# Layer A's attention: the output bank copied once and its crossed halves turned by DMA and added by GpSimd, a long row's minimum carried from one piece to the next, and small operations moved or dropped

## The chip, the cores and the metric

The kernel runs on one core of one Trainium2 chip. A core has five engines with queues of their own: TensorE (PE: matrix products and transposes; PEld is its loading of weights), VectorE (DVE), ScalarE (ACT), GpSimd (POOL) and SyncE (SP), which here issues nearly all DMAs. Each engine works through its queue in order, and an instruction that waits for a semaphore holds up everything behind it on that engine. The metric is the device time of one execution in microseconds, the median of several runs; lower is better.

## What is computed

A causal decoder of two layers on 1024 tokens of width 1024, in float32. Layer A attends in three ways and mixes them by gates; layer B attends with dilated windows over a shared K and V; each layer ends in a SwiGLU feed-forward part. The change lies in layer A's attention alone. Cut to what matters:

```
q: 16 heads of 64, K and V: 4 groups (4 heads share one), scale 1/8
o_cmp = softmax(q k_cmp + bias) v_cmp          # 63 compressed blocks of keys
imp   = sum over the 4 heads of p_cmp, per block of 64 keys
sel   = the 8 best blocks of a query (first, own and previous one forced)
o_sel = softmax(q k[sel] + bias) v[sel]        # causal
o_win = softmax(q k[last 256] + bias) v[last 256]
o     = g0 * o_cmp + g1 * o_sel + g2 * o_win   # g = sigmoid(gate logits)
x     = x + o @ w_out
```

A softmax here takes the row's maximum off first. The kernel keeps negated scores (the factor -1/8 is in q, the bias is stored negated), so the row's maximum is a minimum, and ACT forms exp(minimum - score).

## The kernel before, in words

**Stages.** The program runs through: projections of layer A (to about 290 us), layer A's attention (about 290 to 750), its output projection and feed-forward part (to about 1450), the shared K and V and layer B's queries, layer B's attention (about 1927 to 2230), its output projection and feed-forward part. All products keep float32 accuracy: a value is split into a rounded part (`h`) and the rest (`l`), and two or three fast products take the place of one slow one. Where a tile is used whole, one slow product (line L296) does it.

**Layer A's attention.** The work is cut into 32 units (g, t): 4 groups of heads by 8 blocks of 128 queries, the group on the outside. A unit has five jobs: `cmp_job` (compressed blocks, 4 heads, and for t >= 4 the choice of blocks) and four `dense_job`s: window (br = 2) and selected (br = 1), each for two heads (hp = 0, 1). A job has a front and a back, and `pipelined` puts a job's back two jobs behind its front.

- The front of `dense_job`: PE forms the scores of a head (L675, L676; `s`, three PSUM banks), DVE adds the bias, writes `P` and takes the minimum of the row in one instruction (L678). A row of over 512 keys (br = 1, t >= 4) comes in two pieces, n - 512 and 512 keys; the minima of both go into `mp`, and L682 takes the smaller one. ACT forms the exponentials and their sum (L684), DVE the reciprocal (L686), GpSimd multiplies by it and by the gate (L688).
- The back: PE turns blocks of `P` (L275, `pt`, three banks), ACT copies the result rounded (`th`, L138), DVE forms the rest (`tl`, L139), and PE adds the product with V into the unit's output bank (`o`, two banks; L297, L298). Some blocks go another way, to take load off DVE: a plain copy out of PSUM (L289, by ACT for hp = 0, by DVE for hp = 1), and GpSimd makes `th` and `tl` (L290, L291). And the window's first two blocks for hp = 1 are copied whole (`whole`, L281, by ACT) and used in the slow product L296.
- `cmp_job` has small steps on DVE: the sum is held above 1e-30 (L614), the reciprocal (L615), for t = 0 a mask (L617), the product with the gate (`dg`, L619); GpSimd multiplies `pc` by it (L623).
- At the end of a unit `evac_o` empties the output bank. It holds 64 columns of V's rounded part and 64 of its rest, so that for every second head the two 64-partition halves have to be crossed and added: ACT copies one half of the bank to the other partitions (L308, 64x256), DVE adds the other half to it (L309); both twice per unit. The sum goes into `oT`, which the output projection reads.

**What sets the order.** Instructions are put on the engines by a scheduler that goes by its own costs and by the order in which the program was written; so an edit in one place can move instructions elsewhere. Loads for a group (Q, K, KW, V, VW, T) are issued by SP when a slot of their ring is free, most of them at a change of group. The output projection's weights `ow` and its input `xr` are loaded by the same queue, into memory that the attention gives back.

Of the kernel before, what the change touches and what calls it, by code (L numbers as in the profile page):

```python
# [10 lines left out]
F32 = mybir.dt.float32  # L11
# [3 lines left out]
OP = mybir.AluOpType  # L15
# [76 lines left out]
def trunk(ctx, tc, I, out):  # L92
    nc = tc.nc
# [206 lines left out]
    cp_a, cp_v = nc.scalar.copy, nc.vector.tensor_copy  # L300
# [214 lines left out]
    oT = pool(oT_ctx, "oTa", "right").tile([128, KC, S], F32, name="oT")  # L515

    with ExitStack() as c:
        kB = pool(c, "aB")
        wk = pool(c, "aw")
# [16 lines left out]
        grp = {}  # L536
# [50 lines left out]
        gt = lambda g, t, br, h0, n: gates[:, t, 12 * g + 3 * h0 + br:12 * g + 3 * (h0 + n):3]  # L587
        tok = lambda t: slice(t * 128, (t + 1) * 128)

        def query(g, t, hh):  # L590
            return grp["Q", g, t // 4, hh][:, tok(t % 4)]

        def cmp_job(g, t):
# [17 lines left out]
            for hh in range(4):  # L611
                nc.scalar.activation(pc[:, hh, :nv], pc[:, hh, :nv], AF.Exp, bias=mx[:, hh:hh + 1], scale=-1.0,
                                     accum_out=dn[:, hh:hh + 1])
            nc.vector.tensor_scalar(dn, dn, 1e-30, None, op0=OP.max)  # L614
            nc.vector.reciprocal(dn, dn)  # L615
            if t == 0:
                nc.vector.tensor_scalar(dn, dn, crow, None, op0=OP.mult)  # L617
            dg = wk.tile([128, 4], F32, name="dg", bufs=3)
            nc.vector.tensor_mul(dg, dn, gt(g, t, 0, 0, 4))  # L619
            if t >= 4:  # L620
                pn = wk.tile([128, 4, 64], F32, name="pn", bufs=2)
                nc.gpsimd.tensor_mul(pn[:, :, :nv], pv, dn[:].unsqueeze(2).to_broadcast([128, 4, nv]))
# [25 lines left out]
                nc.tensor.matmul(po, vc[:, g, :], tl, start=False, stop=False, skip_group_check=True)  # L648
            return back

        def dense_job(g, t, br, hp):

            k0 = max(t - 2, 0) if br == 2 else 0
            nb = t + 1 - k0
            n = 128 * nb
            P = wk.tile([128, 2, 1024 if br == 1 else 384], F32, name=f"P{br}", bufs=4)
            mm = wk.tile([128, 2], F32, name="m", bufs=8)
            sm = wk.tile([128, 2], F32, name="sm", bufs=8)
            masked = br == 1 and t >= 4
            kh, kl = grp["K", g] if br == 1 else grp["KW", g, t // 4]  # L660
            skip = 256 if br == 2 and t >= 4 else 0
            cuts = [(0, n - 512, 0), (n - 512, n, 1)] if n > 512 else [(0, n, 1)]
            mp = wk.tile([128, 2, 2], F32, name="mp", bufs=4) if len(cuts) == 2 else None
            for e in range(2):
                hh = 2 * hp + e
                q = query(g, t, hh)
                for i, (lo, hi, a) in enumerate(cuts):
                    bias = grp["T", g, a, hh] if br == 1 else grp["TW", g, hh]
                    ps = bank("s")
                    w, rw = max(hi - lo, 256), hi - lo  # L670
                    ks = slice(k0 * 128 - skip + lo, k0 * 128 - skip + lo + w)

                    nr = 128 if br == 2 else 80 if masked else 64
                    ql = grp["QM", g][:, hh, tok(t - 4)] if masked else q
                    nc.tensor.matmul(ps[:, :w], q, kh[:, ks], start=True, stop=False)  # L675
                    nc.tensor.matmul(ps[:, :w], ql[:nr], kl[:nr, ks], start=False, stop=True)  # L676
                    bs = slice(bias.shape[-1] - rw, bias.shape[-1])
                    nc.vector.tensor_tensor_reduce(  # L678
                        out=P[:, e, lo:hi], in0=ps[:, :rw], in1=bias[:, bs], scale=1.0, scalar=3e38, op0=OP.add,
                        op1=OP.min, accum_out=mm[:, e:e + 1] if len(cuts) == 1 else mp[:, e, i:i + 1])  # L680
            if len(cuts) == 2:
                nc.vector.tensor_tensor(mm, mp[:, :, 0], mp[:, :, 1], op=OP.min)  # L682
            for e in range(2):
                nc.scalar.activation(P[:, e, :n], P[:, e, :n], AF.Exp, bias=mm[:, e:e + 1], scale=-1.0,  # L684
                                     accum_out=sm[:, e:e + 1])
            nc.vector.reciprocal(sm, sm)  # L686
            for e in range(2):
                nc.gpsimd.tensor_scalar(P[:, e, :n], P[:, e, :n], sm[:, e:e + 1], gt(g, t, br, 2 * hp + e, 1),  # L688
                                        op0=OP.mult, op1=OP.mult)

            def back():
                po = po_[g, t]
                for b0 in range(0, nb, 2):
                    bs = range(b0, min(b0 + 2, nb))
                    th, tl = transposed(wk, [P[:, e, b * 128:(b + 1) * 128] for b in bs for e in range(2)],
                                        (cp_a, cp_v)[hp] if br == 2 and b0 == 2 else None,
                                        whole=cp_a if br == 2 and hp == 1 and b0 == 0 else None)
                    for i, b in enumerate(bs):
                        last = br == 1 and b == nb - 1
                        cs = slice(i * 256, (i + 1) * 256)  # L700
                        o_ = po[:, hp * 256:(hp + 1) * 256]
                        v_ = grp["V", br - 1, g, (k0 + b) // 4][:, (k0 + b) % 4, :]
                        mm_pv(o_, v_, th, tl, cs, False, last)
                if br == 1 and hp == 1:
                    evac_o(wk, po, oT[:, 2 * g:2 * g + 2, tok(t)])
            return back

        def jobs():
# [955 lines left out]
```

## Time and profile before

| | us |
|---|---|
| median of 3 runs (lowest, highest) | 3033.9 (3033.78, 3038.08) |
| the profiled execution, first to last instruction | 3035.7 |
| PE, DVE, ACT, POOL busy in it | 2899.3, 2401.7, 1603.6, 1630.1 |
| mean granted TensorE clock | 0.983 |

The page gives no device time of the profiled execution beside its span. The span lies within the spread of the runs, so what lies around it is smaller than that spread.

How to read the views. A row of the groups is: line, engine, operation, what is written and read, count | busy us, mean ns of one | idle us of the engine just before these instructions, and what ended it. A row of the waits is: who waited, for whom, us in total, times, longest us. A row of the windows gives each engine's busy time in a stretch, with the number of instructions. A row of the timeline is: start, duration, engine, line, operation, count, and in brackets the idle time ahead of it. "PEld" rows are loads of weights; since PE's queue is in order, a weight load that waits holds PE up.

### The profile page before, as it was taken

What the parts mean: (1) busy time and instruction counts of PE and PEld (TensorE: products, weight loads), DVE (VectorE), ACT (ScalarE), POOL (GpSimd) and SP (SyncE); (2) the same over time, 40 slices, a digit from 0 to 9 for tenths busy, and PEclk for the clock granted to TensorE, in tenths of its full rate; (3) what the DMA queues carried; (4) which work ended last, traced back from release to release, by engine and by line L of the source; (5) the groups of instructions that cost most, each with busy time, mean ns of one, the idle gap of its engine ahead of it and who ended that gap; (6) DMA issues with size and microseconds to landing.
All of it is one profiled execution on the core that took longest, in us unless ns stands there. A gap on an engine that the chain in (4) does not pass through costs nothing.

```text
span 3035.7 us, 44147 instructions
## 1 busy us (share of the span) xinstructions
PE 2899.3 (96%) x14670; PEld 2381.4 (78%) x14670; DVE 2401.7 (79%) x4832; ACT 1603.6 (53%) x3596; POOL 1630.1 (54%) x1751
## 2 busy tenths in 40 slices
PE   7999999999889999999999999899988899999997
PEld 6987888888677877777777778788866787777776
DVE  4432888988988888888876677589899788888887
ACT  5432888887463333333364444689965433333334
POOL 2134666666766555555556787333357755555551
PEclk9999999999999999999999999999999999999999
DMA  6765032121112222222124555876420211112111
GB/s 167 223 191 165 25 103 78 36 56 70 60 53 63 63 67 74 65 59 70 56 95 141 160 160 145 264 209 179 138 94 25 66 55 57 56 46 62 51 45 73
DMA packets 266196, 293.43 MB, mean 97 GB/s; under 512 B 17971, under 2 KB 209347, under 8 KB 265968
## 3 DMA queue, kind: packets, MB, share of 16 engines
q1 hardware_dynamic: 246320, 230.45, 26.3%
q0 software_dynamic: 19648, 60.16, 6.6%
q8 instruction: 116, 1.90, 0.3%
q14 instruction: 112, 0.92, 0.1%
HBM read 227.44 MB, written 78.81 MB: 101 GB/s over the span
## 4 chain that ended last, share of the span: by engine, by line
PE 68%; DVE 16%; ACT 5%; issue 4%; DMA 4%; POOL 2%; SPq 1%; DVEq 0%; ACTq 0%; POOLq 0%
PE ux L165 5%; PE ux L166 5%; PE ux L167 5%; PE uy L166 4%; PE uy L165 4%; PE uy L167 4%; DVE pl L762 4%; PE pt L275 4%; PE dx L166 3%; PE dr L165 3%; PE dx L167 3%; PE dx L165 3%; PE dr L166 3%; PE dr L167 3%; PE mm L165 3%
## 5 line engine op out<-in xcount | busy, mean ns | idle before, releaser
L762 DVE TENSOR_TENSOR pl<-oT,ph 128x512 fp32r<-128x512 f32 x315 | 325.2, 1052 | 41.3 <-ACT ph L761 35.4
L761 ACT ACTIVATE ph<-oT 128x512 fp32r<-128x512 f32 x329 | 199.0, 626 | 228.1 <-PE ux L166 65.8
L275 PE MATMUL pt<-ident,P 128*128 128x128 f32 x1536 | 245.1, 278 | 11.0 <-ACT P L1458 2.7
L761 ACT ACTIVATE ph<-oTb 128x512 fp32r<-128x512 f32 x239 | 143.2, 625 | 189.4 <-PE ux L166 55.7
L762 DVE TENSOR_TENSOR pl<-oTb,ph 128x512 fp32r<-128x512 f32 x229 | 224.4, 1005 | 23.5 <-ACT ph L761 23.4
L820 DVE TENSOR_TENSOR xr<-xr,dr 128x512 f32<-128x512 f32 x336 | 214.6, 679 | 33.9 <-PE dr L167 33.8
L139 DVE TENSOR_TENSOR tl<-pt,th 128x512 fp32r<-128x512 f32 (+1 forms) x320 | 207.1, 651 | 33.8 <-ACT th L138 31.9
L820 DVE TENSOR_TENSOR xr<-xr,dx 128x512 f32<-128x512 f32 x352 | 220.3, 678 | 3.6 <-PE dx L167 2.4
L166 PE MATMUL dx<-pl,ph 128*128 128x512 f32 x512 | 203.4, 401 | 9.7 <-DVE pl L762 9.0
L688 POOL TENSOR_SCALAR P<-P,sm,gates 128x384 f32<-128x384 f32 (+7 forms) x256 | 183.5, 728 | 53.4 <-DVE sm L686 48.0
L275 PEld LDWEIGHTS pt<-ident,P 128*128 128x128 f32 x1536 | 179.8, 142 | 30.0 <-ACT P L1458 6.7
L138 ACT ACTIVATE th<-pt 128x512 fp32r<-128x512 f32 (+1 forms) x320 | 177.2, 563 | 44.3 <-PE pt L275 40.4
L167 PE MATMUL dx<-ph,pl 128*128 128x512 f32 x512 | 200.0, 397 | 0.3 <-DVE pl L762 0.3
L684 ACT ACTIVATE P<-P,m 128x384 f32<-128x384 f32 (+7 forms) x256 | 170.7, 669 | 16.1 <-DVE m L682 8.4
L1081 POOL TENSOR_TENSOR oT<-oT,gffn 128x512 f32<-128x512 f32 x92 | 105.9, 1158 | 136.2 <-DMA oT<-in_ffn_w_up_dram 110.5
L165 PE MATMUL dx<-ph 128*128 128x512 f32 x512 | 157.3, 400 | 6.7 <-DVE xr L820 3.3
L1081 POOL TENSOR_TENSOR oTb<-oTb,gffn 128x512 f32<-128x512 f32 x92 | 106.4, 1165 | 99.1 <-DMA oTb<-in_ffn_w_up_dram 77.0
L298 PE MATMUL o<-tl,V 128*128 128x256 f32 x540 | 148.8, 299 | 7.4 <-POOL tl L291 3.7
L297 PE MATMUL o<-th,V 128*128 128x256 f32 x540 | 151.4, 296 | 2.7 <-ACT th L138 1.4
L290 POOL TENSOR_SCALAR th<-traw 128x128 fp32r<-128x128 f32 (+1 forms) x112 | 75.1, 674 | 129.3 <-ACT traw L289 47.7
L1458 ACT ACTIVATE P<-P,st 128x384 f32<-128x384 f32 (+2 forms) x256 | 139.6, 547 | 7.6 <-PE pt L1569 4.1
L166 PEld LDWEIGHTS dx<-pl,ph 128*128 128x128 f32 x512 | 97.6, 191 | 39.5 <-DVE pl L762 19.4
(617 smaller groups left out, 9582.4 us busy)
## 6 DMA issues: line engine op xcount, KB each, us to landing
qB<-xr POOLq DMA_DIRECT2D x96, 256.0 KB, 4.7
oT<-in_ffn_w_up_dram SPq DMA_DIRECT2D x92, 256.0 KB, 3.0
oTb<-in_ffn_w_up_dram SPq DMA_DIRECT2D x92, 256.0 KB, 3.0
Q<-qB SPq DMA_DIRECT2D x40, 512.0 KB, 7.0
wd<-in_ffn_w_down_dram SPq DMA_DIRECT2D x66, 256.0 KB, 2.6
oT<-in_b_w_q_dram SPq DMA_DIRECT2D x48, 256.0 KB, 3.5
K<-kBs SPq DMA_DIRECT2D x40, 256.0 KB, 9.5
wraw<-in_a_w_in_dram SPq DMA_DIRECT2D x18, 512.0 KB, 4.9
```

The costliest lines, as they stand in the source:

```text
L138: nc.scalar.activation(H_, src, AF.Copy)
L139: nc.vector.tensor_sub(L_, src, f32(H_))
L165: nc.tensor.matmul(ps, lh, rh, start=first, stop=False, skip_group_check=bool(shared))
L166: nc.tensor.matmul(ps, lh, rl, start=False, stop=False, skip_group_check=bool(shared))
L167: return nc.tensor.matmul(ps, ll, rh, start=False, stop=last, skip_group_check=bool(shared))
L275: nc.tensor.transpose(ps[:, i * 128:(i + 1) * 128], b, ident)
L684: nc.scalar.activation(P[:, e, :n], P[:, e, :n], AF.Exp, bias=mm[:, e:e + 1], scale=-1.0, accum_out=sm[:, e:e + 1])
L688: nc.gpsimd.tensor_scalar(P[:, e, :n], P[:, e, :n], sm[:, e:e + 1], gt(g, t, br, 2 * hp + e, 1), op0=OP.mult, op1=OP.mult)
L761: nc.scalar.activation(h, src, AF.Copy)
L762: (eng or nc.vector).tensor_sub(l, src, f32(h))
L820: nc.vector.tensor_add(xs, xs, banks[t])
L1081: nc.gpsimd.tensor_mul(v, v, gains[:, k:k + 4].unsqueeze(2).to_broadcast([128, 4, 128]))
```

## The change

Five edits, all in layer A's attention:

1. `evac_shifted` takes the place of `evac_o` (which layer B keeps). ACT copies the whole bank to SBUF in one instruction (`oraw`, 128x512, one buffer); SP issues two DMAs of 64x256 that put each crossed half on its partitions (`oturn`, two buffers); GpSimd adds each half (64x256, both inputs in SBUF) into `oT`.
2. A row of two pieces: the minimum of the first piece is the start value of the second piece's instruction, so that its result is the row's minimum. L682 is gone. The pieces are now on the outside of the loop and the two heads inside.
3. `dg` is formed by GpSimd.
4. The bound of 1e-30 is kept for t = 0 only.
5. The whole copy of the window's first two blocks (hp = 1) goes from ACT to DVE.

```diff
-            nc.vector.tensor_scalar(dn, dn, 1e-30, None, op0=OP.max)
+            if t == 0:
+                nc.vector.tensor_scalar(dn, dn, 1e-30, None, op0=OP.max)
             nc.vector.reciprocal(dn, dn)
...
-            nc.vector.tensor_mul(dg, dn, gt(g, t, 0, 0, 4))
+            nc.gpsimd.tensor_mul(dg, dn, gt(g, t, 0, 0, 4))
...
+        def evac_shifted(po, dst):
+
+            raw = wk.tile([128, 2, 2, 128], F32, name="oraw", bufs=1)
+            turn = wk.tile([128, 2, 128], F32, name="oturn", bufs=2)
+            nc.scalar.copy(raw, po[:].rearrange("p (c e q) -> p e c q", e=2, q=128))
+            for e in range(2):
+                own, oth = slice(64 * e, 64 * e + 64), slice(64 - 64 * e, 128 - 64 * e)
+                nc.sync.dma_start(turn[own], raw[oth, e])
+                nc.gpsimd.tensor_add(dst[own], raw[own, e], turn[own])
...
-            mp = wk.tile([128, 2, 2], F32, name="mp", bufs=4) if len(cuts) == 2 else None
-            for e in range(2):
-                hh = 2 * hp + e
-                q = query(g, t, hh)
-                for i, (lo, hi, a) in enumerate(cuts):
-                    bias = grp["T", g, a, hh] if br == 1 else grp["TW", g, hh]
+            part = wk.tile([128, 2], F32, name="mp", bufs=4) if len(cuts) == 2 else None
+            bias = lambda e, a: grp["T", g, a, 2 * hp + e] if br == 1 else grp["TW", g, 2 * hp + e]
+            for i, (lo, hi, a) in enumerate(cuts):
+                for e in range(2):
+                    hh = 2 * hp + e
+                    q = query(g, t, hh)
...
-                    bs = slice(bias.shape[-1] - rw, bias.shape[-1])
+                    b_ = bias(e, a)
+                    last = i == len(cuts) - 1
                     nc.vector.tensor_tensor_reduce(
-                        out=P[:, e, lo:hi], in0=ps[:, :rw], in1=bias[:, bs], scale=1.0, scalar=3e38, op0=OP.add,
-                        op1=OP.min, accum_out=mm[:, e:e + 1] if len(cuts) == 1 else mp[:, e, i:i + 1])
-            if len(cuts) == 2:
-                nc.vector.tensor_tensor(mm, mp[:, :, 0], mp[:, :, 1], op=OP.min)
+                        out=P[:, e, lo:hi], in0=ps[:, :rw], in1=b_[:, b_.shape[-1] - rw:], scale=1.0,
+                        scalar=part[:, e:e + 1] if i else 3e38, op0=OP.add, op1=OP.min,
+                        accum_out=(mm if last else part)[:, e:e + 1])
...
-                                        whole=cp_a if br == 2 and hp == 1 and b0 == 0 else None)
+                                        whole=cp_v if br == 2 and hp == 1 and b0 == 0 else None)
...
-                    evac_o(wk, po, oT[:, 2 * g:2 * g + 2, tok(t)])
+                    evac_shifted(po, oT[:, 2 * g:2 * g + 2, tok(t)])
```

Since the scheduler sets the order, the edits also move instructions. The rows below are word for word the queues as the two programs have them; numbers in names tell buffers apart. From line 700 of the old kernel on, the new one's lines are 11 higher (L688 is now L699, L1051 is L1062).

GpSimd's queue at the end of the third group, between the scaling of two rows; before:

```order
L688 TENSOR_SCALAR P_7635<-P_7635,sm,gates 128x384 x2
L623 TENSOR_TENSOR pc_2488<-pc_2488,dg 128x4x63
L626 MEMSET a_8868 128x68
L290 TENSOR_SCALAR th<-traw 128x256
L604 MEMSET pc_2487 128x4x57
L291 TENSOR_TENSOR tl<-traw,th 128x256
L290 TENSOR_SCALAR th<-traw 128x256
L688 TENSOR_SCALAR P_7675<-P_7675,sm,gates 128x896 x2
```

The same place after (L660 is the new addition):

```order
L699 TENSOR_SCALAR P_7638<-P_7638,sm,gates 128x384 x2
L627 MEMSET a_8872 128x68
L290 TENSOR_SCALAR th<-traw 128x256
L604 MEMSET pc_2487 128x4x57
L291 TENSOR_TENSOR tl<-traw,th 128x256
L660 TENSOR_TENSOR oT<-oraw,oturn 64x2x128 x2
L699 TENSOR_SCALAR P_7678<-P_7678,sm,gates 128x896 x2
L558 AFFINE_SELECT TW_6437<-T_6435 128x384
L290 TENSOR_SCALAR th<-traw 128x256
```

Both additions stand between one `tl` and the next row's scaling, and the next `th` has moved behind that scaling.

SP's queue at the change from the first to the second group, the loads of K and V of the next groups; before:

```order
L268 DMA K_4604<-kS 64x1024
L569 DMA K_4605<-kS 64x1024
L570 DMA K_4605<-bS 16x1024
L580 DMA VW_4337<-vS 128x4x128
L580 DMA V_4351<-vS 128x4x128
L580 DMA V_4610<-vS 128x4x128
```

The same place after:

```order
L268 DMA K_4604<-kS 64x1024
L569 DMA K_4605<-kS 64x1024
L570 DMA K_4605<-bS 16x1024
L659 DMA oturn<-oraw 64x256 x2
L580 DMA VW_4336<-vS 128x4x128
L580 DMA V_4350<-vS 128x4x128
L580 DMA V_4610<-vS 128x4x128
L659 DMA oturn<-oraw 64x256 x4
```

The turned halves stand between and behind the large loads.

SP's queue at the end of the attention, with the loads for the output projection; before:

```order
L1051 DMA ow_9973<-in_a_w_out_dram 128x1024
L1051 DMA ow_9975<-in_a_w_out_dram 128x1024
L1051 DMA ow_9977<-in_a_w_out_dram 128x1024
L1051 DMA ow_9971<-in_a_w_out_dram 128x1024
L1054 DMA ow_9974<-in_a_w_out_dram 128x1024
L1053 DMA xr<-in_x_dram 128x1024 x2
```

And after:

```order
L1062 DMA ow_9977<-in_a_w_out_dram 128x1024
L1062 DMA ow_9979<-in_a_w_out_dram 128x1024
L659 DMA oturn<-oraw 64x256 x2
L1062 DMA ow_9981<-in_a_w_out_dram 128x1024
L1062 DMA ow_9975<-in_a_w_out_dram 128x1024
L1065 DMA ow_9978<-in_a_w_out_dram 128x1024
```

Three of the five weight tiles that were ahead of `xr` now stand behind the last unit's halves. In layer B's attention, whose code is as it was, the scheduler also deals a part of the rows out in another order.

## The prediction

> **What bounds the kernel now.** I read the page's first part, then the window of layer A's attention, then who waited for whom in it, and last the groups of instructions that the change touches. First the page and the stage as a whole (the columns of the second row are the stretch, its length, busy us of PE, PEld, DVE, ACT and POOL with counts, granted clock, DMA share, GB/s):
>
> ```profile
> span 3035.7 us, 44147 instructions
> 286.00:752.00 466.00, 449.23 (x2938) 386.87 (x2937) 395.29 (x1599) 388.69 (x1133) 302.20 (x492) 0.98 0.21 60
> ```
>
> All edits lie in these 466 us. PE is busy for 449 of them and idle for 17. DVE is at 85%, ACT at 83%, POOL at 65%. So PE is the bound, with two engines close behind it, and an edit that takes work off DVE or ACT gains only what PE now waits for them. The waits of PE's weight loads in the stage show for whom (total us, times, longest):
>
> ```profile
> PEld o L298 <- DVE tl L139: 8.0, 20, 0.7
> PEld s L675 <- DVE m L678: 7.9, 18, 0.9
> PEld o L298 <- POOL tl L291: 3.4, 8, 0.8
> PEld pt L640 <- DVE mk L638: 2.3, 3, 0.8
> PEld pt L275 <- DVE tl L139: 1.7, 5, 0.6
> PEld s L600 <- DVE mp L678: 1.7, 4, 0.4
> PEld o L297 <- POOL th L290: 1.1, 2, 0.9
> PEld o L298 <- DVE m L678: 1.1, 6, 0.2
> ```
>
> Six rows name DVE: 8.0 + 7.9 + 2.3 + 1.7 + 1.7 + 1.1 = 22.7 us, in many small pieces: a score bank that DVE has not emptied, a `tl` that is not ready. Two name POOL: 4.5 us, both for its `th`/`tl`. None names POOL's scaling of P (L688), so a late scaling does not reach PE. DVE is thus where a gain can come from: at most 23 us, 0.75% of the program.
>
> PE's busy row alone leaves 466 - 449 = 17 us of room, less than the named waits of 22.7 and 4.5 together, so it counts some waiting as work; I go by the waits, which also say whose lateness costs. [...]
>
> **The change part by part.** These groups are touched, from the groups in the window 290 to 750 (count | busy us, mean ns | idle before):
>
> ```profile
> L309 DVE TENSOR_TENSOR oT<-o,ot 64x256 f32<-64x256 f32 x62 | 25.9, 418 | 2.6 <-ACT ot L308 1.8
> L308 ACT ACTIVATE ot<-o 64x256 f32<-64x256 f32 x63 | 23.9, 379 | 4.3 <-PE o L298 2.8
> L281 ACT COPY traw<-pt 128x512 f32<-128x512 f32 x28 | 16.4, 584 | 3.1 <-PE pt L275 2.9
> L281 ACT COPY traw<-pt 128x256 f32<-128x256 f32 x4 | 1.5, 373 | 1.4 <-PE pt L275 1.4
> L139 DVE TENSOR_TENSOR tl<-pt,th 128x512 fp32r<-128x512 f32 x188 | 127.8, 684 | 22.9 <-ACT th L138 22.6
> L289 DVE COPY traw<-pt 128x256 f32<-128x256 f32 x24 | 9.9, 411 | 0.6 <-POOL tl L291 0.5
> L682 DVE TENSOR_TENSOR m<-mp 128x2 f32<-128x2 f32 x32 | 8.4, 263 | 0.1
> L619 DVE TENSOR_TENSOR dg<-cd,gates 128x4 f32<-128x4 f32 x32 | 8.3, 261 | 0.3
> L614 DVE TENSOR_SCALAR cd<-cd 128x4 f32<-128x4 f32 x32 | 7.7, 240 | 3.6 <-ACT pc L612 3.6
> L291 POOL TENSOR_TENSOR tl<-traw,th 128x256 fp32r<-128x256 f32 x48 | 35.3, 736 | 0.8
> L623 POOL TENSOR_TENSOR pc<-pc,dg 128x252 f32<-128x252 f32 x4 | 2.4, 606 | 0.1
> L623 POOL TENSOR_TENSOR pc<-pc,dg 128x28 f32<-128x28 f32 x4 | 0.9, 234 | 2.4 <-ACT th L138 1.6 <-DVE dg L619 0.8
> ```
>
> *DVE.* Gone: 64 additions, 64 x 0.418 = 26.8; L682, 8.4; `dg`, 8.3; 28 bounds, 28 x 0.240 = 6.7. New: 28 whole copies of 128x512 out of PSUM, which the trace does not show on DVE; L139 reads the same bank in 0.684, and L289 copies half of it in 0.411, so it lies between 0.62 (0.411 and ACT's step of 0.21 from 256 to 512 wide) and 0.68; I take 0.68, the nearest in shape: 28 x 0.68 + 4 x 0.41 = 20.7. PE's L296 then waits for DVE where it waited for ACT, two engines about equally busy; no price. Net -29.5: DVE falls from 395 to 366 us, 79%. The start value of the minimum as a pointer costs nothing that I can price; a chain on an instruction two before it on the same engine bounds it by L682's own 0.26 each, 8 us, and by zero below (it cannot gain). I take zero, since an instruction of the other head stands between.
>
> *ACT.* Gone: 64 x 0.379 = 24.3 and 17.9 of whole copies. New: 32 copies of 128x512, by L281's row 32 x 0.584 = 18.7. Net -23.5: 389 to 365, 78%. The output bank comes free after one copy instead of two copies and two additions. The copy needs the one `oraw` buffer back from the additions of the unit before, with exponentials queued behind it; units are 466 / 32 = 14.6 us apart and copy, landing and additions take some 5, so it won't wait.
>
> *POOL.* New: 64 additions of 64x256 with both inputs in SBUF. L623 at 252 wide takes 0.606, L291 at 256 takes 0.736; I take 0.70: 45. `dg`: 32 x 0.234 by the 28-wide form = 7.5. POOL goes from 302 to 354, 76%, waits aside. In its queue `dg` waits for DVE's reciprocal and stands ahead of `pc`, which waited for DVE there before. Could POOL's additions slow DVE? L139 takes 0.684 in a stage where POOL is busy 65% of the time; its one big input is in PSUM, as L678's is. Two inputs in SBUF do suffer (L762, below), but such instructions on DVE are small here. No price.
>
> *SP and the DMAs.* 64 DMAs of 64 KB. SP now waits at each pair for ACT's copy, and behind it stand the loads; POOL waits at each addition for the landing, and behind it stand the scalings (no matter) and the next `th`/`tl` (which PE waits for). What POOL does with its time now:
>
> ```profile
> POOL P L688 <- DVE sm L686: 48.0, 39, 3.6
> POOL th L290 <- ACT traw L289: 18.6, 9, 4.8
> K<-kS SPq DMA_DIRECT2D x9, 256.0 KB, 9.1
> K<-bS SPq DMA_DIRECT2D x3, 64.0 KB, 8.8
> VW<-vS SPq DMA_DIRECT2D x6, 256.0 KB, 2.8
> ```
>
> POOL idles 466 - 302 = 164 us, 5.1 per unit, mostly for inputs of a scaling or a `th`. The additions take 1.4 + 0.2 of the 5.1 and leave 3.5 for waits. The last three rows are landings (KB, median us from issue): 2.8 on a quiet queue, 8.8 for 64 KB behind the other K loads. I take 2.8 as the usual landing. [...]
>
> *The sum in the stage.* The 22.7 us that PE waits for DVE fall as DVE comes to have more room. If they go with the inverse of DVE's idle time (71 us before, 100 after), they fall to 16, a gain of 7; all of them gone is the end, 23; none is the other end. I take 11, nearer the former, with something for the exponentials, which no longer wait for L682:
>
> ```profile
> ACT P L684 <- DVE m L682: 8.4, 13, 1.9
> ```
>
> POOL's 4.5 us, by the same rule, 164 to 112 us of idle time, become 6.6: 2 us lost; with the waits at the additions from 0 to 20 us (the rival below).
>
> *The end of the stage.* Here the last half is late for the output projection, and three weight tiles move behind ACT's last copy:
>
> ```profile
> 734.55 0.42 SPq L1054 DMA_DIRECT2D ow<-in_a_w_out_dram  x1
> 749.66 0.38 ACT L308 ACTIVATE ot<-o 64x256 f32<-64x256 f32 x1 [1.43 <-PE o L298]
> 751.82 3.48 POOL L828 TENSOR_TENSOR ta<-oT 128x512 f32<-128x512 f32 x2 [5.16 <-DVE oT L309]
> 755.77 1.78 DVE L762 TENSOR_TENSOR pl<-oT,ph 128x512 fp32r<-128x512 f32 x1
> 756.12 0.62 PE L165 MATMUL dr<-ph 128*128 128x512 f32 x2
> 755.00:760.00 5.00, 5.00 (x23) 4.10 (x22) 5.00 (x4) 2.31 (x4) 5.00 (x4) 0.96 1.03 417
> ```
>
> The fifth weight tile, issued at 734.55 before, would be issued at about 752 and, at 417 GB/s 1.26 us a tile, land near 758, where PE first uses it at 756.1: 2 us late. Against that, POOL stood idle 5.2 us for `oT` before; its queue after has two sums of weights ahead of the last halves, and so fewer of its sums beside DVE's L762, which takes 1.78 next to them and 0.69 alone (750.59 in the same view). I take +1, between -2 and +4.
>
> ```profile
> 750.59 0.69 DVE L762 TENSOR_TENSOR pl<-oT,ph 128x512 fp32r<-128x512 f32 x1
> 2000.00:2080.00 80.00, 75.87 (x571) 68.61 (x571) 71.89 (x244) 72.78 (x218) 24.13 (x42) 1.00 0.69 196
> ```
>
> Layer B's attention is dealt out anew in part. There PE is idle for 4.1 of 80 us; over its 300 us that makes some 16, and a quarter of it either way is 4. I take 0.
>
> Sum: -11 + 2 + 1 = -8 us. The span of the profiled execution, 3035.7, lies among the runs (3033.78 to 3038.08), so I take the difference off their median: 3033.9 - 8 = 3026. What is late next is POOL: at 76% with waits in its queue it is as near to PE as DVE.
>
> **The rivals.**
>
> *No change.* DVE's waits go, and POOL's take their place, for PE needs `th`/`tl` from both. For it: POOL's rise of 52 us is more than DVE's fall of 29.5. Against: 48 `tl` come from POOL (L291) and 188 wide ones from DVE (L139), so DVE's lateness reaches PE more often. It gives 3034, within 6 us.
>
> *Slower: the halves land late at the changes of group.* At each of the three changes, K, T, Q and V fill the DMA queue, and two or three units' halves stand behind them in SP's queue. If such a half lands after 8.8 instead of 2.8 us, POOL stands 6 us longer, 2.5 past its room, with the next `th` behind it. Seven or eight such units at 2.5 us are 19 us of PE; with the gain of 11 and the +3 it comes to +11: 3045. The places stand in the chain of work that ended last:
>
> ```profile
> 387.30 4.33 DMA T<-sA
> 499.62 3.76 DMA T<-sA
> 612.33 2.92 DMA T<-sA
> ```
>
> It decides once a landing exceeds about 6 us, the 2.8 and 3.5 together. For it: the K rows. Against: halves whose copy comes late meet a queue already emptied.
>
> *Far faster.* All named waits on DVE go: -23 + 3 = -20, 3014. Against: at 79% DVE will still be late at times.
>
> **How the numbers follow.** A measurement of this kernel tells about 0.2%, 6 us, from no change. The forecast, 3026, gets 0.37; far faster 0.08; no change 0.26; slower 0.29, of which the greater part within 3045. At their bounds the parts give -23 (DVE) - 2 (end) - 4 (layer B) and 0 + 20 (POOL) + 4 + 4 + 8 (pointer), which will not all meet; the range that leaves out some 2 in 10 reaches to the far gain and to the slower rival: 3012 to 3046. Cases of both signs hold most of the chance: the forecast's own range is 3018 to 3028. Faster 0.45, same 0.26, slower 0.29.
>
> **What would show it right or wrong.** In the profile after: DVE near 366 us in the stage, ACT 365, POOL 354; PE's waits for DVE at 10 to 16 us; its waits for POOL's `th`/`tl` under 8; POOL's waits at the additions under 3.5 us each. Additions that wait over 6 us at 380 to 400, 490 to 510 and 600 to 620, with PE waiting for `tl`, would show the slower rival. The prediction is wrong if PE's waits for DVE stay at 20, or if the stage is shorter and the time is lost behind 750 us.

## The result and the profile after

The changed kernel takes 3061.4 us (median of 4 runs, 3057.6 to 3064.8) against 3036.0 (4 runs beside them): the ratio is 1.0073, 95% interval 1.0055 to 1.0091, so it is slower by about 22 us. The prediction said 3026, with a range of 3012 to 3046. The profiled execution took 3057.6 us on the device, 1.9 more than its span.

The page's first line, and then the windows' row of the stage, up to the first product of the output projection (751.7 us before, 773.2 after):

```profile
span 3055.7 us, 44333 instructions
```

```profile
286.00:773.20 487.20, 453.86 (x2936) 390.13 (x2934) 370.46 (x1474) 363.87 (x1069) 351.94 (x587) 0.96 0.23 61
```

The stage is longer by 21.5 us, the span by 20.0; layer B's attention is shorter by 1.7. So the loss lies in layer A's attention, although DVE, ACT and GpSimd are busy there within 5 us of what was worked out (366, 365, 354). The waits of the stage (290 to 772 us):

```profile
ACT P L695 <- DVE m L690: 31.2, 47, 1.6
ACT th L138 <- POOL tl L291: 24.6, 13, 3.6
POOL oT L660 <- DMA oturn<-oraw: 15.6, 19, 2.0
PEld o L298 <- POOL tl L291: 13.3, 16, 2.5
PEld o L297 <- POOL th L290: 12.7, 9, 3.3
PEld s L686 <- DVE m L690: 9.6, 19, 1.1
PEld o L298 <- DVE tl L139: 2.5, 6, 0.5
```

The group of the new additions, and the issues of their transfers:

```profile
L660 POOL TENSOR_TENSOR oT<-oraw,oturn 64x256 f32<-64x256 f32 x62 | 45.1, 727 | 24.6 <-DMA oturn<-oraw 15.6 <-ACT th L138 3.7 <-ACT pc L612 1.6
```

```profile
oturn<-oraw SPq DMA_DIRECT2D x62, 64.0 KB, 2.0
```

PE waits 26.0 us for GpSimd's `th` and `tl` instead of 4.5. ACT now waits for GpSimd too (24.6 us): its own `th` come from the same ring of four buffers as GpSimd's, and a late pair keeps them. The loss comes in steps at the changes of group: the output bank of the last unit of each of the four groups is copied 2.9, 12.5, 17.6 and 21.8 us later than before. PE has five stops of 1.9 us or more ahead of a pair `th`/`tl`, ending at 402.0, 515.0, 519.6, 637.0 and 751.0 us; all but the second are at pairs of hp = 1. The second and third are shown here, at the change from the second to the third group. GpSimd's timeline there, then the transfers that the first additions wait for, then PE's two stops, then the windows of 4 us:

```profile
505.87 2.39 POOL L699 TENSOR_SCALAR P<-P,sm,gates 128x1024 f32<-128x1024 f32 x2
...
508.60 0.86 POOL L290 TENSOR_SCALAR th<-traw 128x256 fp32r<-128x256 f32 x1
509.40 0.41 POOL L561 COPY C<-T 128x32 f32<-128x32 f32 x2
512.68 1.51 POOL L660 TENSOR_TENSOR oT<-oraw,oturn 64x256 f32<-64x256 f32 x2 [2.87 <-ACT th L138]
514.27 0.72 POOL L291 TENSOR_TENSOR tl<-traw,th 128x256 fp32r<-128x256 f32 x1
514.98 3.23 POOL L699 TENSOR_SCALAR P<-P,sm,gates 128x1024 f32<-128x1024 f32 x4
...
518.69 0.85 POOL L290 TENSOR_SCALAR th<-traw 128x256 fp32r<-128x256 f32 x1
```

```profile
L659 SPq DMA_DIRECT2D oturn<-oraw x2: 482/540/598, 506.9 to 507.5; - x2
DMA to landing us min/median/max: 5.4/5.5/5.6
```

```profile
515.05 0.39 PE L298 MATMUL o<-tl,VW 128*128 128x256 f32 x1 [2.26 <-POOL tl L291]
519.59 0.58 PE L297 MATMUL o<-th,VW 128*128 128x256 f32 x1 [2.04 <-POOL th L290]
```

```profile
508.00:512.00 4.00, 4.00 (x30) 3.45 (x28) 2.70 (x19) 4.00 (x20) 1.81 (x6) 1.00 0.95 246
512.00:516.00 4.00, 1.74 (x7) 1.25 (x7) 0.97 (x3) 1.11 (x4) 3.16 (x4) 0.97 1.05 226
516.00:520.00 4.00, 1.97 (x8) 1.29 (x7) 1.40 (x3) 0.60 (x1) 4.00 (x10) 0.50 0.73 177
520.00:524.00 4.00, 4.00 (x19) 3.66 (x19) 1.77 (x7) 1.74 (x6) 2.21 (x5) 0.50 0.00 0
524.00:528.00 4.00, 4.00 (x26) 3.64 (x26) 0.76 (x3) 1.16 (x3) 0.00 (x0) 0.75 0.01 4
```

Two additions and the 2.9 us ahead of them part a `th` from its `tl`, at a pair of hp = 0. The row puts the 2.9 us down to ACT's `th`, but an addition reads `oraw` and `oturn` alone: the first half, issued at 506.9, landed 5.6 us later, at 512.5, and the addition began at 512.68. So here GpSimd stands for a late half, and the slower rival's mechanism is behind this one stop. The next `th`, of hp = 1, stands behind four scalings of 1024 columns. PE, which at a change of group has only short rows ahead, is busy 3.7 of 8 us. And from 515.8 to 526.0 us the granted clock is 0.50 (the 0.97 and 0.75 are means over 4 us), and what follows goes more slowly as well: PE's products with V (L297 and L298, 128x256) take 0.41 us each from 522 to 524 us, and 0.28 at 529.6 and 529.7 us, at a clock of 1.00. Summing (1 - clock) x 4 us over all windows of 4 us from 288 us to the stage's end gives 10.2 us before and 18.8 after; summing what PE is not busy gives 16.8 and 33.3. The two rises, 8.6 and 16.5, come within 4 us of the 21.5; they come to more since the clock is also low while PE stands (0.50 from 516 to 520 us, with PE busy for 1.97 of the 4), so 8.6 is an upper estimate for the clock. The same sum meets the stage's change in each of the 18 runs below to within 7 us.

### The profile page after: what moved, and what is told of

It reads as the page before. It is cut to its first block, busy times and chain, and to the rows that moved or that the text cites. A ratio compares the mean times of both kernels' runs of the same rounds, so it can differ in the third digit from the quotient of the medians.

```text
span 3055.7 us, 44333 instructions
## 1 busy us (share of the span) xinstructions
PE 2898.8 (95%) x14670; PEld 2380.4 (78%) x14670; DVE 2367.4 (77%) x4708; ACT 1579.2 (52%) x3532; POOL 1675.3 (55%) x1847
## 4 chain that ended last, share of the span: by engine, by line
PE 67%; DVE 13%; ACT 6%; issue 5%; POOL 4%; DMA 3%; SPq 1%; DVEq 0%; POOLq 0%; ACTq 0%
PE ux L165 6%; PE ux L166 5%; PE ux L167 5%; PE uy L166 4%; PE uy L165 4%; PE uy L167 4%; DVE pl L773 4%; PE pt L275 3%; PE dr L165 3%; PE dr L166 3%; PE dx L166 3%; PE dr L167 3%; PE dx L167 3%; PE dx L165 3%; DVE xr L831 3%
## 5 line engine op out<-in xcount | busy, mean ns | idle before, releaser
L699 POOL TENSOR_SCALAR P<-P,sm,gates 128x384 f32<-128x384 f32 (+7 forms) x256 | 182.4, 723 | 49.1 <-DVE sm L697 41.6
L695 ACT ACTIVATE P<-P,m 128x384 f32<-128x384 f32 (+7 forms) x256 | 171.6, 672 | 32.9 <-DVE m L690 31.2
L297 PE MATMUL o<-th,V 128*128 128x256 f32 x540 | 151.6, 300 | 6.1 <-POOL th L290 3.1
L298 PE MATMUL o<-tl,V 128*128 128x256 f32 x540 | 148.1, 299 | 2.0 <-DVE tl L139 1.4
L166 PEld LDWEIGHTS dx<-pl,ph 128*128 128x128 f32 x512 | 97.0, 189 | 39.3 <-DVE pl L773 19.5
```

Of the source, the lines that this page charges most:

```text
L166: nc.tensor.matmul(ps, lh, rl, start=False, stop=False, skip_group_check=bool(shared))
```

## The experiments

Each run is compared with the kernel before on the same chip (3037 to 3039 us). In the table: the ratio with its interval, the ratio as us of 3038, all waits of PE's weight loads in the stage that name GpSimd, and GpSimd's busy time in the stage. The last two columns are of one execution each, the profiled one; run 2's took 3045.5 us, where its median is 3053.8.

| run | what it is | ratio [95%] | us | PE for GpSimd | GpSimd busy |
|---|---|---|---|---|---|
| | before | 1 | 0 | 4.7 | 302 |
| | after | 1.0073 [1.0055, 1.0091] | +22 | 26.2 | 352 |
| 1 | edits 2 to 5 | 1.0015 [1.0003, 1.0028] | +5 | 5.3 | 307 |
| 2 | edit 1 alone | 1.0043 [1.0026, 1.0059] | +13 | 12.2 | 349 |
| 3 | 2 to 5, additions bunched | 1.0106 [1.0083, 1.0129] | +32 | 18.1 | 346 |
| 4 | after, additions on DVE | 1.0060 [1.0041, 1.0079] | +18 | 7.4 | 315 |
| 5 | 2 to 5, additions' work only | 1.0083 [1.0065, 1.0100] | +25 | 15.1 | 342 |
| 6 | 2 to 5, waits for halves only | 1.0033 [1.0020, 1.0046] | +10 | 7.1 | 316 |
| 7 | after, t = 6, 7 the old way | 1.0051 [1.0034, 1.0068] | +15 | 24.0 | 340 |
| 8 | edits 2, 3, 4 | 1.0011 [0.9998, 1.0023] | +3 | 7.6 | 305 |
| 9 | after, hp = 1 pair off GpSimd | 0.9954 [0.9939, 0.9969] | -14 | 3.6 | 318 |
| 10 | after, hp = 0 pair off GpSimd | 1.0062 [1.0040, 1.0084] | +19 | 15.8 | 317 |
| 11 | edit 2 | 1.0001 [0.9988, 1.0013] | 0 | 5.1 | 301 |
| 12 | edits 3, 4 | 1.0045 [1.0031, 1.0060] | +14 | 7.2 | 309 |
| 13 | before, hp = 1 pair off GpSimd | 1.0025 [1.0013, 1.0038] | +8 | 3.2 | 264 |
| 14 | run 5, hp = 1 pair off GpSimd | 0.9997 [0.9983, 1.0011] | -1 | 2.4 | 305 |
| 15 | edit 3 | 1.0001 [0.9986, 1.0015] | 0 | 2.5 | 305 |
| 16 | edit 4 | 1.0074 [1.0052, 1.0097] | +22 | 13.4 | 300 |
| 17 | after, pair ahead of scalings | 1.0128 [1.0111, 1.0145] | +39 | 20.3 | 351 |
| 18 | edit 4, hp = 1 pair off GpSimd | 1.0001 [0.9991, 1.0012] | 0 | 1.6 | 264 |

Several runs came out beyond every range that was written down for them: runs 3, 5, 12, 13, 16 and 17 higher, run 9 lower; runs 1 and 6 lie between two ranges.

**Runs 1 and 2: edit 1 undone, and alone.** Theory 1: GpSimd's new work and waits make its `th`/`tl` late. Rivals: the transfers (2), the order of the pieces (3), the whole copy on DVE (4). The call of `evac_shifted` is exchanged:

```diff
-                    evac_shifted(po, oT[:, 2 * g:2 * g + 2, tok(t)])
+                    evac_o(wk, po, oT[:, 2 * g:2 * g + 2, tok(t)])
```

> The changed kernel with the old way of emptying the output bank (evac_o); edits 2 to 5 stay. Theory 1 (GpSimd's queue: the 64 additions, 45 us, and its waits for the halves put the scalings and th/tl behind, above all at the three changes of group): GpSimd falls back to about 308 us busy in 290 to 770 us, PE's waits for its th/tl from 26 us to below 8, and the time to 3022 to 3036 us. Theory 2 (the halves' transfers and SP's queue): the same here. Theory 3 (the order of the pieces in edit 2 makes ACT's exponentials wait) or theory 4 (the whole copy on DVE): the time stays at 3050 to 3061.

> The kernel before with edit 1 alone: the bank copied once, halves turned by DMA, GpSimd adds. Theories 1 and 2: 3050 to 3066 us, PE stopped for 3 to 5 us at the three changes of group with the granted clock at about half behind it. Theory 3 or 4: 3028 to 3038, since DVE loses 27 us of work and nothing else changes.

Undoing edit 1 takes back 18 of the 22 us, and edit 1 alone loses 13, so theories 3 and 4 fall as the main cause. But run 1 misses its 3022 to 3036: edits 2 to 5 gain nothing by themselves. PE's waits moved to DVE there, which got the whole copies:

```profile
PEld s L686 <- DVE m L690: 16.2, 24, 1.5
PEld o L297 <- POOL th L290: 4.1, 5, 1.5
PEld o L298 <- POOL tl L291: 1.2, 3, 0.7
```

**Runs 3, 5 and 6: the work without the wait, the wait without the work.** Run 3's additions depend on nothing, and the scheduler put all 64 between 291 and 399 us, so it doesn't answer its question; the loss arose just there (23 us by the eighth unit). Run 5 makes them depend on each unit's sum; run 6 has the transfers and a copy of 64x1 that waits for them (the first line below is run 5's, the others run 6's; all of them only add to the kernel of run 1):

```diff
+                nc.gpsimd.tensor_add(idle[own], dst[own], dst[own])
...
+                nc.sync.dma_start(turn[own], tmp[own])
+                nc.gpsimd.tensor_copy(idle[own], turn[own, 0, 0:1])
```

> The changed kernel with evac_o, and beside it two additions of 64x256 on GpSimd per unit that read a constant tile and write a tile that nobody reads: GpSimd's 45 us are there, the waits for halves and the transfers are not. Theory 1 in the form that the work itself is too much: 3045 to 3061. Theory 1 in the form that the wait ahead of the additions does it (GpSimd's queue stands still for it), or theory 2: within 5 us of the run with evac_o alone.

> The run with evac_o (edits 2 to 5; 3042 us) with two additions of 64x256 on GpSimd per unit that read what the unit has just put into oT and write a tile that nobody reads, so that they are spread over the stage (in the third run all 64 stood in its first 110 us, which alone made it lose): about 40 us of work for GpSimd, no transfer. Theory 1a (GpSimd's work itself makes its scalings and th/tl late): 3050 to 3060. Theory 1b/2 (only the wait for the half, or the transfer): 3042 plus or minus 4.

> The run with evac_o and the two transfers of 64 KB per unit: the half that ACT has copied is sent over other partitions by SP, and GpSimd copies one column of it (64x1) into a tile that nobody reads, so it waits for the landing in its queue but has little work. The sum is made by DVE as before. Theory 1a: 3042 to 3047. Theory 1b/2 (GpSimd standing still for a landing, above all in the bursts of loads at a change of group): 3050 to 3062, the loss in steps at the three changes.

In run 6 GpSimd stands 54.7 us for halves, more than in the change, at a cost of 5 us over run 1, about as much as the two intervals allow by chance. In run 5 38 us of work cost 20. The wait of run 6, then the group of the additions in run 5, then PE's waits in run 5:

```profile
POOL idle L662 <- DMA oturn<-ot: 54.7, 43, 2.9
```

```profile
L660 POOL TENSOR_TENSOR idle<-oT 64x256 f32<-64x256 f32 x63 | 38.4, 609 | 18.5 <-DVE oT L659 14.0 <-DVE sm L699 2.0 <-DVE mk L639 0.2
```

```profile
PEld o L297 <- POOL th L290: 10.7, 9, 2.2
PEld o L298 <- POOL tl L291: 3.9, 8, 0.8
```

So the work, not the landing, seems the greater part. (Run 5's order differs from run 1's as well; run 16 shows what that can be worth.)

**Run 4: the additions on DVE.**

```diff
-                nc.gpsimd.tensor_add(dst[own], raw[own, e], turn[own])
+                nc.vector.tensor_add(dst[own], raw[own, e], turn[own])
```

> The changed kernel with the 64 additions on DVE in place of GpSimd; copy and transfers as in the change. Theory 1: GpSimd at about 309 us busy, PE's waits for th/tl below 8 us, and 3022 to 3040 us. Theory 2 (a half that comes late holds up whoever adds it): the waits move to DVE, which everyone waits for, and the time stays at 3050 or goes above 3061.

Here the transfers do matter. GpSimd is relieved, and yet the time stays at +18, in three steps at the changes of group. DVE's timeline at the first, and the windows of 4 us behind it:

```profile
398.15 0.54 DVE L660 TENSOR_TENSOR oT<-oraw,oturn 64x256 f32<-64x256 f32 x1 [4.62 <-DMA oturn<-oraw]
```

```profile
396.00:400.00 4.00, 0.79 (x4) 0.41 (x3) 1.78 (x9) 1.19 (x6) 4.00 (x7) 0.89 1.07 266
400.00:404.00 4.00, 4.00 (x13) 2.78 (x12) 2.51 (x12) 2.38 (x10) 0.95 (x5) 0.50 0.50 139
404.00:408.00 4.00, 4.00 (x18) 3.62 (x17) 0.53 (x2) 0.60 (x1) 1.65 (x5) 0.50 0.02 4
```

With the 16 DMA engines full of the next group's loads (1.07), DVE stands 4.6 us for the first half with the score banks behind it, PE stops for 3.2 us, and the clock is 0.50 from 399.1 to 409.4 us. At the second change the two halves land 6.9 us after their issue (median).

**Run 7: the old way at the last two units of a group.**

```diff
-                    evac_shifted(po, oT[:, 2 * g:2 * g + 2, tok(t)])
+                    (evac_crossed if t >= 6 else evac_shifted)(po, oT[:, 2 * g:2 * g + 2, tok(t)])
```

> The changed kernel in which the last two units of each group (t = 6, 7) are emptied the old way and the other 24 units the new way. If the loss arises at the changes of group, from whichever cause in edit 1 (additions and waits that stand ahead of the last unit's scalings of 1024 columns): 3038 to 3048, no step at the changes. If it is spread over all units: it falls by a quarter of the 19 us that edit 1 costs, to about 3056.

At 3054.9 us (+15) it is near the 3056 of a loss spread over all units, and PE still waits 24 us for GpSimd. So the additions of the last units alone are not the cause.

**Runs 9 and 10: the same relief for GpSimd at two places.** In a unit with t >= 2 GpSimd makes two pairs `th`/`tl`, one of hp = 0 and one of hp = 1. I followed them through the trace by their buffers, from the end of the copy L289 to the end of L291. For hp = 1 this takes 3.4 us on average before, 5.4 after, 5.4 in run 2 and 3.4 in run 1; for hp = 0 2.7 before and 3.4 after. And of the 26.0 us that PE's weight loads wait for a pair in the stage after, 22.4 are at pairs of hp = 1 and 3.6 at hp = 0. The back of the window's hp = 1 is written behind the fronts of both selected-branch jobs, so four scalings of up to 1024 columns stand near it in GpSimd's queue. Each run takes one of the pairs off GpSimd:

```diff
-                                        (cp_a, cp_v)[hp] if br == 2 and b0 == 2 else None,
+                                        (cp_a, None)[hp] if br == 2 and b0 == 2 else None,     # run 9
+                                        (None, cp_v)[hp] if br == 2 and b0 == 2 else None,     # run 10
```

> The changed kernel, whole, with GpSimd relieved of as much work as edit 1 gave it: for hp = 1 the third block's th and tl are made by ACT and DVE as for the other blocks, so that 24 pairs of L290 and L291 (1.58 us each, 38 us) leave GpSimd; DVE loses the plain copy and forms tl (0.42 for 0.41), ACT gains 24 roundings (about 8 us). Transfers, waits for halves and the order of pieces stay. If GpSimd's total work sets the loss: GpSimd at about 315 us, PE's waits for th/tl below 8 us, 3034 to 3044. If the waits for halves or edit 2 set it: 3052 to 3061.

> The same for hp = 0: 24 pairs leave GpSimd, ACT rounds in place of copying (no change), DVE gains 24 differences of 128x256 (10 us; 370 to 380). GpSimd's work as the cause: 3034 to 3044, near the run for hp = 1; halves or order as the cause: 3052 to 3061.

GpSimd is busy 318 and 317 us. One run gains 14 us over the kernel before, the other loses 19. PE's waits in run 9, then in run 10, and GpSimd's timeline in run 10 at the second change of group:

```profile
PEld s L686 <- DVE m L690: 9.4, 16, 0.8
PEld o L297 <- POOL th L290: 1.8, 2, 1.6
PEld o L298 <- POOL tl L291: 1.6, 3, 0.6
```

```profile
PEld o L297 <- POOL th L290: 11.2, 6, 3.5
PEld o L298 <- POOL tl L291: 4.6, 7, 1.5
```

```profile
512.03 0.23 POOL L563 COPY C<-T 128x31 f32<-128x31 f32 x1 [5.17 <-DMA T<-sA]
512.35 0.72 POOL L660 TENSOR_TENSOR oT<-oraw,oturn 64x256 f32<-64x256 f32 x1
513.04 0.85 POOL L290 TENSOR_SCALAR th<-traw 128x256 fp32r<-128x256 f32 x1
```

So GpSimd's total of work is not what decides; theory 1 in that form falls. The loss goes with the hp = 1 pair: with what stands ahead of it in GpSimd's queue, and (run 16 below) with what PE has to do meanwhile. At this place in run 10 a copy that waits 5.2 us for a load, and an addition, stand ahead of it: the pair's blocks were copied at 507 us, PE stopped for 3.2 us ahead of its `th`, and its `tl` was ready 12.0 us after the copy.

**Runs 13, 14 and 18: the same cut elsewhere.** The line of run 9 in the kernel before, in run 5, and in run 16 (edit 4 alone).

> The kernel before with the cut of run 9 alone: the third block's th and tl for hp = 1 by ACT and DVE. GpSimd 302 - 38 = 264 us, ACT +8 to 397, DVE the same at 395. PE waits only 4.5 us for GpSimd's th/tl in the kernel before. If the loss is carried by GpSimd's hp = 1 pair under the change's load: 3030 to 3040, no gain worth speaking of, and run 9's gain belongs to the change and the cut together. If the cut is a gain by itself: 3018 to 3028, and the change is worth nothing even with it.

> The run with GpSimd's work alone (3066 us) with the same cut for hp = 1. GpSimd's pair for hp = 1 as the carrier: 3035 to 3046, near the run with evac_o (3042). The work itself wherever it stands: 3050 to 3060.

> Edit 4 alone (3060 us) with the cut for hp = 1, which takes the pair off GpSimd. If edit 4 alone loses through that pair, pushed behind other work by a new order: 3036 to 3046, as the kernel before with the cut (3045). If it loses through DVE's own order (pieces of tl behind small steps that wait for GpSimd): 3050 to 3060.

Without the cut these four kernels stand at 0, +25, +22 and (the change) +22; with it at +8, -1, 0 and -14. The cut is no gain by itself (3045 us, above both ranges written down for run 13); it takes away what the others lose. With the pair off GpSimd the change is worth -14 - 8 = -22 us against the kernel before with the same cut. I put that down to the work taken off DVE and ACT: PE's waits for DVE, all rows, are 22.5 us in run 9 and 35.4 in run 13, those for ACT 8.0 and 15.4. No run parts it from the new order. Run 9, at 3024.7 us, is the best kernel of the study.

**Runs 8, 11, 12, 15 and 16: edits 2, 3 and 4 apart.** Each is the kernel before with the edits named.

> Edits 2, 3 and 4 alone: evac_o, and the whole copy with ACT as before. DVE 395 - 20 = 375 us busy in layer A's attention, ACT unchanged at about 389. If DVE's load sets PE's waits, as the prediction took it: 3024 to 3034, below before. Theory 3 (the order of the pieces makes the exponentials wait for both heads' last pieces): 3038 to 3046, as with edit 5.

> The kernel before with edit 2 alone (pieces outside, heads inside, the minimum carried; L682 gone). DVE -8.4 + 3.6 = -5 us. If the order of the pieces costs what edits 3 and 4 save: 3043 to 3050. If edit 2 is harmless: 3034 to 3041, the same as before.

> The kernel before with edits 3 and 4 alone: DVE -8.3 - 6.7 = -15 us, GpSimd +6.5. If DVE's load sets PE's waits: 3028 to 3035. If each microsecond given to GpSimd costs about half of one (24 us for the 39 us of the load-only run) and DVE's relief is worth nothing: 3041 to 3044.

> The kernel before with dg on GpSimd and nothing else. If edit 3 carries the 13.6 us of edits 3 and 4: 3046 to 3054. If it is harmless: 3032 to 3042.

> The kernel before with the bound kept for t = 0 only and nothing else: 28 operations of 0.24 us less on DVE. By arithmetic it can only gain: 3028 to 3036. If it loses (3042 to 3054), what it moves is the order that the scheduler writes, since it takes work away and adds none.

Edit 2 alone 0, edit 3 alone 0, edit 4 alone +22, 3 and 4 together +14, all three +3: they don't add up. Since edit 2 alone costs nothing, theory 3 has no part in it. Edit 4 only takes 28 small operations from DVE, yet PE waits 13.4 us for GpSimd's pairs, and runs 16 and 18 say that the loss goes with them: PE's waits for DVE rise as well in run 16 (39.3 us, 27.7 before), but in run 18 they are still 34.8 and the time is that of before. The longest of run 16's stops for a pair is at the last change of group. That stop, run 16's windows there, and the windows of the kernel before at the same pair:

```profile
620.58 0.39 PE L297 MATMUL o<-th,VW 128*128 128x256 f32 x1 [2.38 <-POOL th L290]
```

```profile
616.00:620.00 4.00, 2.20 (x12) 1.67 (x11) 3.25 (x7) 3.98 (x16) 4.00 (x6) 1.00 1.00 259
620.00:624.00 4.00, 3.19 (x12) 2.71 (x13) 2.11 (x6) 1.30 (x3) 2.70 (x5) 0.67 0.05 14
```

```profile
616.00:620.00 4.00, 4.00 (x31) 3.73 (x30) 3.61 (x21) 3.95 (x9) 2.05 (x5) 1.00 0.91 235
620.00:624.00 4.00, 4.00 (x22) 2.90 (x21) 2.87 (x13) 4.00 (x20) 3.94 (x6) 1.00 0.28 56
```

The pair of hp = 1 is no slower here: from its copy to the end of `tl` it takes 5.8 us in the kernel before and 5.6 in run 16. But before, PE has 31 and 22 instructions of other jobs to do meanwhile; in run 16 it has 12 and 12, and it stops. So a new order, with no work added, can cost as much as the whole change, and at this place it does so by taking away what PE does while it would wait.

**Run 17: the pair put ahead of the scalings.** All work of the change stays; the scalings of the selected branch's hp = 1 are written into the window's back and made to follow the pair.

```diff
+                while br == 2 and hp == 1 and behind:
+                    with after(pair[0] if nb > 2 else None):
+                        behind.pop(0)()
```

> The changed kernel with all of its work, in another order: the two scalings of the selected branch's hp = 1 must follow the unit's hp = 1 pair (L290, L291) in GpSimd's queue. If it is the pair's place in the queue that costs: PE's waits for th/tl of hp = 1 from 16 us to below 6, and 3030 to 3048. If it is GpSimd's total work, or if the scalings are needed as soon as the pair: PE waits for the scalings in place of the pair, and 3052 to 3070.

It lost 39 us. PE's waits name the scalings for 0.2 us only. At hp = 1 PE's own stops did fall, from 15.3 us in the change to 5.9, as the first expectation had it; but those at hp = 0 rose from 2.8 to 8.0, as here (L293 is L291, L565 is L563, L300 is L298), and its weight loads still wait 19.9 us for the pairs. Their waits for DVE rose too, from 20.7 to 30.3 us; what caused that was not tested. GpSimd's timeline, then PE's:

```profile
520.50 0.23 POOL L565 COPY C<-T 128x31 f32<-128x31 f32 x1 [3.53 <-DMA T<-sA]
...
521.80 0.72 POOL L293 TENSOR_TENSOR tl<-traw,th 128x256 fp32r<-128x256 f32 x1
```

```profile
522.58 0.58 PE L300 MATMUL o<-tl,VW 128*128 128x256 f32 x1 [2.58 <-POOL tl L293]
```

So moving the scalings away from the pair is not enough: additions, scalings and copies that wait for a load take each other's place. That the change loses through GpSimd's pairs, those of hp = 1 above all, is shown by one cut in four kernels (runs 9, 13, 14, 18, with run 10 against it); each of these runs also has an order of its own, and whether some order would let the change gain with the pairs on GpSimd is left open.

## Why the prediction was wrong

- *What the edits add and remove on each engine*: right. 64 additions took 0.727 us (0.70 taken), the copies of the bank 0.584 (0.584), the whole copies on DVE 0.682 (0.68), `dg` 0.203 (0.234). The pointer as a start value is not free: 0.741 us against 0.68, some 4 us, inside its bound.
- *The landings*: right as a rule (median 2.0 us, 2.8 taken). The slower rival's 8.8 us at all three changes did not come: only the pair of halves issued at 507 us was late, 5.6 and 5.4 us, and the wait for it (2.9 us) is behind one of PE's five long stops. Its end, 3045, was too low, and by run 6 (5 us) its mechanism carries little here; with DVE as the adder it shows at all three changes (run 4).
- *PE's waits for DVE fall by 11 us*: the same six rows fell from 22.7 to 15.8, by 7, and all rows that name DVE from 27.7 to 20.7. That is the 7 which the rule of inverse idle time gave, but it may be luck: in runs 8, 12 and 15, with DVE 5 to 10 us less busy than before, these waits rose to 29.5, 34.7 and 31.3 us, and the time did not fall. ACT's wait for the minimum, expected to go with L682, doubled: 31.2 us, where the two rows of before (L682 and L678) held 15.1.
- *POOL's 4.5 us "by the same rule ... become 6.6"*: this is the step that failed. They became 26.0, a loss of 21.5 us where 2 were taken. The rule of inverse idle time treats a queue as if its work arrived by chance. GpSimd's queue is served in order (at the change from the second to the third group a `tl` began at 514.27 us, behind 2.87 us of waiting and 1.51 us of two additions), and the additions push the pair of hp = 1 back among the scalings that already stood around it: its `tl` is ready 5.4 us after the copy on average, 3.4 before (and 3.4 in run 1, without the additions). Of PE's 26.0 us 22.4 are waits for these pairs, with the long stops at the changes of group, where PE has little else to do. The rows of the changed order showed the second `th` behind the two scalings of 896 columns and the additions; the prediction priced the additions' waits there (0 to 20 us) but not their place.
- *"The scalings (no matter)"*: right for PE's own waits (no row names them), wrong for the pair behind them.
- *What was not in the sum*: the clock. The granted clock of 0.50 behind PE's longer stops cost up to 8.6 us more, an estimate from the windows of 4 us.
- *"Layer B ... I take 0"*: near (-1.7).
- *"I take +1", the end of the stage*: too low, though inside its bounds of -2 and +4. ACT waited 6.31 us for a weight tile (`ow`) that now comes behind the last halves, and the first product `dr` came at 780.62 us against 756.12: 24.5 us later than before, 3.0 more than the stage's end. At layer B's first scores the lag is still 23.5 us; in layer B's attention and behind it, it falls to the 20.0 us of the span.
- *The range* took each cost from its own bounds and had no term for a new order. Run 16 puts one at 22 us.

## What to carry to other kernels

Before work is moved to an engine with idle time, find in its queue the instruction that the bounding engine needs soonest, and count what will stand ahead of it and what the bounding engine can do meanwhile; the share of busy time says nothing about that (runs 9 and 10, 318 and 317 us busy, differ by 33 us). Where a scheduler writes the order, any edit deals it anew: here a small gain by arithmetic came out only together with a cut that took the instruction with the least slack (the least time to spare before PE waits for it) out of that queue, and a range for such an edit has to hold an order that is 20 us worse. A stop of PE can cost more than its length by the clock (in the change it was 0.50 for 10.2 us from just behind the stop of 2.26 on, with one of 2.04 among them), but no fixed share goes with it: beside a rise of PE's idle time of 16.5 us the clock's sum rose by 8.6 in the change, in run 4 by 12.0 beside 12.0, in run 16 by 1.7 beside 14.3.

## What the runs showed of the hardware

- The granted clock fell to 0.50 beside stops of PE. In the change PE's five stops of 1.90 to 3.07 us end at 402.0, 515.0, 519.6, 637.0 and 751.0 us, and the clock was 0.50 from 403.1 to 406.5, from 515.8 to 526.0, from 638.6 to 642.0 and from 751.3 to 754.7. In run 16 it was 0.50 from 621.3 to 624.8, behind the stop of 2.38 that ends at 620.58 (the 0.67 is a mean over 4 us); in run 4 from 399.1 to 409.4, where the stop of 3.21 ends at 399.55. Far shorter stops had it behind them too: in the kernel before it was 0.50 from 335.6 to 339.0 us, behind two of 0.61 and 0.52, and from 731.5 to 734.9, behind one of 0.47.
- A small DVE sum with two inputs in SBUF took far longer once beside GpSimd's work. In run 12 a sum of 128x16 took 1.82 us while GpSimd ended two scalings and ran a product and a `tl`; it ended with that `tl`, and two `tl` of DVE's own stood behind it. In the kernel before the same 16 sums (L632) took 0.16 us at the shortest, 0.21 in the median and 0.65 at the longest. DVE's timeline, then GpSimd's:

```profile
681.86 1.82 DVE L633 TENSOR_TENSOR sc<-sc,force 128x16 f32<-128x16 f32 x1
683.72 1.02 DVE L139 TENSOR_TENSOR tl<-pt,th 128x512 fp32r<-128x512 f32 x2
```

```profile
681.10 1.32 POOL L689 TENSOR_SCALAR P<-P,sm,gates 128x384 f32<-128x384 f32 x2
682.38 0.50 POOL L624 TENSOR_TENSOR pc<-pc,dg 128x188 f32<-128x188 f32 x1
...
682.93 0.73 POOL L291 TENSOR_TENSOR tl<-traw,th 128x256 fp32r<-128x256 f32 x1
```

- Standing still for transfers and working did not cost the same: 54.7 us of waiting on GpSimd cost 5 us of time in run 6, where 38 us of work on the same engine cost 20 (run 5); one wait of 4.6 us on DVE stopped PE for 3.2 (run 4).
